# Tiles 4 and 5 load their first operands into the MLP's row rooms, and tiles 6 and 7 multiply in three passes

## The chip, the cores and the metric

The kernel runs on one core of one Trainium2 chip. The metric is the device time of one execution in microseconds (us). An execution taken by the profiler also has a span, from its first to its last instruction. TensorE (PE) multiplies, with a left operand loaded as weights (PEld); VectorE (DVE), ScalarE (ACT) and GpSimd (POOL) do the elementwise work; SyncE's queue (SP) issues nearly all loads and stores.

## The reference

One transformer block on a sequence of 1024 rows of width 1024, fp32 in and out. The hybrid mixer in the middle is left out here, since the change doesn't touch it.

```python
o   = hybrid_mixer(rms_norm(x, norm1_g), ...)        # two kinds of attention, [1024, 1024]
x   = x + o @ w_out                                  # w_out [1024, 1024]
h   = rms_norm(x, norm2_g)
q   = rms_norm((h @ w_xq).reshape(1024, 4, 128), xq_norm_g)      # 4 heads of 128
p   = softmax(q @ k.T * 128 ** -0.5)                 # k, v: 256 rows of a memory
x   = x + (p @ v).reshape(1024, 512) @ w_xo
h   = rms_norm(x, norm3_g)
out = x + square(relu(h @ w_ff_in)) @ w_ff_out       # inner width 4096
```

## The kernel before

The rows are eight tiles of 128. A first part projects them; then the attention of the tiles runs one after the other, and a second stream of work (`fill`) is laid between its instructions: the memory's keys and values, `between` for tiles 0 and 1 and for 2 and 3, the MLP of tiles 0 to 3 (`mlp`), and `between` for tiles 4 and 5. `between` is all that stands from the attention's rows to the MLP: it loads attention's rows o from DRAM (L948), multiplies them with w_out in four column chunks of 256, adds x (L938), norms (L311, L315), transposes the normed rows (L292), multiplies with w_xq in two chunks, each followed by the memory attention of its two heads (L984 to L1034), and multiplies with w_xo (L1044).

When attention is through, what is left of `between` for tiles 4 and 5 is merged with `between` for tiles 6 and 7; the latter uses a pool of its own, `d2`, opened in the room that attention leaves. After both comes `mlp_tail`, the MLP of tiles 4 to 7. Within each engine a scheduler of the framework then sets the order of the instructions, by its own model of times and by data dependences; an engine works through its list strictly in that order, SyncE's queue too.

There are two ways to multiply fp32. *Whole*: one matmul of fp32 operands, which the trace shows as two records. *Three passes*: both operands are split into a high part hi and a rest lo of a faster type, and hi·hi, hi·lo and lo·hi are added up, three matmuls of one record each. A weight piece is split by `split_w`: ScalarE copies hi (L251), GpSimd or VectorE subtracts to get lo (L256); at the tail these two take turns. Rows are split on the way out of PSUM by `split_ps` (L242 on ScalarE, L243 on VectorE). `between` multiplies whole for tiles 4 to 7; the MLP goes in three passes.

Tiles in SBUF come from rings: a tag with a number of buffers. In the pool of tiles 0 to 5 (`dn`) the tags `b4`, `whi` and `wlo` have four buffers each, and the MLP of tiles 0 to 3 uses the same ones as `between`: `b4` holds its residual rows until they are stored to the output (L1135), `whi` and `wlo` its split weights, `wraw` the raw ones. The MLP's transposed input rows lie in two rooms of their own, `xh` and `xl`, of 16 KB per partition each; after the last feature matmul nothing reads them.

Of the kernel before, what the change touches and what calls it, by code (L numbers as in the profile page):

```python
# [33 lines left out]
KG = 2  # L34
# [4 lines left out]
    "p2": {"x4": 5, "st": 2, "relu": 2, "whi": 4, "wlo": 4, "c8": 3, "c4": 1, "kraw": 4, "pc": 2},  # L39
    "dn": {"b4": 4, "h": 8, "relu": 2, "wraw": 2, "whi": 4, "wlo": 4},  # L40
    "res": {"b4": 4, "g": 2},
    "d2": {"b4": 2, "h": 8, "relu": 2, "whi": 4, "wlo": 4},
    "d3": {"h": 16, "relu": 2, "wraw": 4, "whi": 10, "wlo": 10},
}
PSUMS = {"p1": {"D": 4, "M": 3, "C": 1}, "main": {"S": 2, "PT": 2, "PV": 1, "D": 2, "M": 1}}
# [124 lines left out]
def build(nc, tc, I, C, out):  # L170
# [19 lines left out]
    def ring(pool, tag, shape, dt=F32):  # L190
        n = RINGS[pool.name if isinstance(pool.name, str) else "dn"][tag]
        return pool.tile(shape, dt, tag=tag, name=tag, bufs=n)
# [48 lines left out]
    def split_ps(src, hi, lo):  # L241
        s.activation(hi, src, AF.Copy)  # L242
        v.tensor_tensor(lo, src, hi, op=ALU.subtract)  # L243
# [74 lines left out]
    def weights(pool, xs, nk, wsrc, parts):  # L318

        w = sum(n for _, n in parts)  # L320
        for k0 in range(0, nk, KG):
            kn = min(KG, nk - k0)
            srcs, o = [], 0
            for c0, n in parts:
                srcs.append((lambda r, o=o, n=n: r[:, :, o:o + n],
                             wsrc[k0 * P:(k0 + kn) * P, c0:c0 + n].rearrange("(k p) n -> p k n", p=P)))
                o += n
            ws = load_w(pool, [P, kn, w], *srcs) if len(xs) == 2 else load_whole(pool, [P, kn, w], *srcs)
            for k in range(kn):
                yield [x[:, k, :] for x in ws]  # L330

    def gemm(pool, xs, nk, nt, wsrc, chunks, consume, begun=None):

        for ci, parts in enumerate(chunks):
            w = sum(n for _, n in parts)
            gr = begun if ci == 0 and begun else list(weights(pool, xs, nk, wsrc, parts))
            for t in range(nt):
                pt = pst(TAGS[pool.name][0], [P, w])
                for k in range(nk):
                    if len(xs) == 1:  # L340
                        mm(pt, xs[0](t, k), gr[k][0], k == 0, k == nk - 1)
                        continue
                    wh, wl = gr[k]
                    xh, xl = xs[0](t, k), xs[1](t, k)
                    mm(pt, xh, wh, k == 0, False)
                    mm(pt, xh, wl, False, False)
                    mm(pt, xl, wh, False, k == nk - 1)
                consume(ci, t, pt)
                yield nk * (5 - len(xs)) * w / 2400.0

    def row_by_row(pool, xs, nk, nt, wsrc, chunks, consume):

        gs = [list(weights(pool, xs, nk, wsrc, parts)) for parts in chunks]
        for t in range(nt):
            for ci, (parts, gr) in enumerate(zip(chunks, gs)):
                yield from gemm(pool, [lambda _, k, x=x, t=t: x(t, k) for x in xs], nk, 1, wsrc, [parts],
                                lambda c, u, pt, ci=ci, t=t: consume(ci, t, pt), gr)

    def xT(pool, nt, whole=False):

        parts = [pool.tile([P, DM // P, nt * P], F32 if whole else F32R, tag="x" + n, name="x" + n)
                 for n in ("h" if whole else "hl")]
        return (parts, [lambda t, k, x=x: x[:, k, t * P:(t + 1) * P] for x in parts],
                lambda t: [x[:, :, t * P:(t + 1) * P] for x in parts])
# [35 lines left out]
    def project(pool, part, late, st):  # L400
# [89 lines left out]

        def w_in(chunks, first, begun=None):
            return gemm(pool, xf, DM // P, nt, W["w_in"], chunks,
                        lambda ci, t, pt: consume(ci + first, t, pt), begun)

        def consume_kv(ci, t, pt):
            s.activation(kraw[t][:, DSA, :], pt[:, :64], AF.Copy)
# [441 lines left out]
            v.tensor_tensor(dst, pt, dst, op=ALU.add)  # L938
        return add_to

    def between(pool, t0, nt, x2s, keep, res=None, then=None):

        o_of = [ring(pool, "b4", [P, 8, P]) for t in range(nt)]
        rows, four = [lambda t, k: o_of[t][:, k, :]], [[(c * 256, 256)] for c in range(4)]
        first = list(weights(pool, rows, 8, W["w_out"], four[0]))
        for t in range(nt):
            for c in (1, 0):
                nc.sync.dma_start(o_of[t][:, c * 4:c * 4 + 4, :], oT_dr[t0 + t][c])  # L948
        x2 = [ring(res or pool, "b4", [P, DM]) for t in range(nt)]
        for t in range(nt):  # L950
            nc.sync.dma_start(x2[t], I["x"][0, (t0 + t) * P:(t0 + t + 1) * P, :])
        add_to = residual_add(x2)
        yield from gemm(pool, rows, 8, nt, W["w_out"], four, add_to, first)
        _, xf, xt_of = xT(pool, nt, True)

        gb2 = gain2(pool, W["norm2_g"])
        for t in range(nt):
# [1 line left out]
            yield 1.0  # L959

        kx, pts = [], {}
        xo = ring(pool, "b4", [P, 4, nt * P])

        def consume_q(ci, t, pt):
            if t == 0:
# [48 lines left out]
        def memory_values(ci, us, prs):  # L1014

            vh, vl = kx[1]
            n = len(us) * P
            split = []
            for h in range(2):
                p2 = pst(TAGS[pool.name][1], [P, 2, n])  # L1020
                for k in range(2):
                    for i, t in enumerate(us):
                        te.transpose(p2[:, k, i * P:(i + 1) * P], prs[t][:, h, k * P:(k + 1) * P], ident)
                ph, pl = ring(pool, "h", [P, 2, n], F32R), ring(pool, "h", [P, 2, n], F32R)
                split_ps(p2, ph, pl)
                split.append((ph, pl))
            pv = pst(TAGS[pool.name][0], [P, 2, n])
            for h, (ph, pl) in enumerate(split):
                hs = slice(h * P, (h + 1) * P)
                for k in range(2):  # L1030
                    mm(pv[:, h, :], vh[:, k, hs], ph[:, k, :], k == 0, False)
                    mm(pv[:, h, :], vl[:, k, hs], ph[:, k, :], False, False)
                    mm(pv[:, h, :], vh[:, k, hs], pl[:, k, :], False, k == 1)
            s.activation(xo[:, ci * 2:ci * 2 + 2, us[0] * P:us[0] * P + n], pv, AF.Copy)  # L1034

        yield from gemm(pool, xf, 8, nt, W["w_xq"], [[(0, 256)], [(256, 256)]], consume_q)

        if not keep and "res" in late:
# [3 lines left out]
            def add_to(ci, t, pt):  # L1042
                cs = slice(ci * 256, (ci + 1) * 256)
                v.tensor_tensor(kept[t][:, cs], pt, x2[t][:, cs], op=ALU.add)  # L1044
        by_tile = [lambda t, k: xo[:, k, t * P:(t + 1) * P]]
        last = (row_by_row if "res" in late else gemm)(pool, by_tile, 4, nt, W["w_xo"], four, add_to)
        yield from alternate(last, then()) if then else last
        for t in range(nt):
# [230 lines left out]
    def fill():  # L1279
        for part in range(1, len(PARTS)):  # L1280
            with tc.tile_pool(name="p2", bufs=1, reuse_waits="tile") as p2:
                yield from project(p2, part, late, st)
            projected.append(part)
        dn = dn_pool.__enter__()
        yield from memory(dn)
        yield 1, PACES[1]
        yield from between(dn, 0, 2, {}, False)
        yield 3, PACES[2]
        x2s, made = {}, {}
        yield from between(dn, 2, 2, x2s, True, None, lambda: pre_norms(dn, made, x2s))  # L1290
        yield 3, PACES[3]
        yield from mlp(dn, 0, 4, x2s, made)
        yield 5, PACES[4]
        yield from between(dn, 4, 2, late["x2s"], False)

    rest = fill()
    together(attend(aw, st), rest, projected)
# [41 lines left out]
```

## Time and profile before

| | us |
|---|---|
| median of 3 runs | 1752.03 (1748.72 to 1753.07) |
| profiled execution | 1755.7 |
| its span | 1753.9 |
| PE busy | 1671.0, 95% of the span |
| ACT busy | 1078.4, 61% |
| DVE busy | 967.4, 55% |
| POOL busy | 923.6, 53% |
| mean granted clock of PE | 0.98 of full |

The times in the rows are us from the start of the span, busy times are us and means of one instruction are ns. An instruction that had to wait shows in brackets how long its engine stood idle before it, and which instruction or DMA ended that. MLP of tiles 0 to 3 ends near 1216, attention near 1272, and the last stage, `mlp_tail`, takes over PE from about 1374 to the end.

### The profile page before, as it was taken

The page shows a single profiled execution, that of the slowest core. Times are in us where ns is not written, and L with a number is a line of the kernel's source. Part 1 is how long each engine was busy: PE and PEld are TensorE (multiplying, and loading weights), DVE is VectorE, ACT ScalarE, POOL GpSimd, SP SyncE. Part 2 cuts the span into 40 slices and gives each one's busy share as a digit, 9 for nine tenths or more (in the row PEclk, how much of TensorE's full clock was granted, in tenths as well). Part 3 has the DMA queues.
Part 4 walks back from the last instruction along what each step waited for, and adds up shares of the span by engine and source line. Part 5 has one row for each costly group of instructions (what it writes and reads, how often), then busy time and mean ns, then how long its engine had stood idle before and what let it go on. Part 6 is the DMA issues. An engine that isn't in the chain of part 4 may idle for free.

```text
span 1753.9 us, 27941 instructions
## 1 busy us (share of the span) xinstructions
PE 1671.0 (95%) x9294; PEld 1447.2 (83%) x9294; DVE 967.4 (55%) x2378; ACT 1078.4 (61%) x2713; POOL 923.6 (53%) x1073
## 2 busy tenths in 40 slices
PE   6998999899999999999999999998989899999999
PEld 6997987788788787888888888887978787888888
DVE  4565668766785886665657555554424544222243
ACT  5444796894698689857995589853313554333344
POOL 2354456554562445686667676673122565444456
PEclk9998999999999999999999999999999999999999
DMA  7434221545145221222122222125474454333353
GB/s 205 122 127 119 70 60 69 189 115 170 52 137 175 73 87 59 65 70 77 61 77 66 65 79 74 56 69 167 146 253 129 148 158 124 96 96 97 97 163 121
DMA packets 169520, 192.21 MB, mean 110 GB/s; under 512 B 24608, under 2 KB 134944, under 8 KB 169376
## 3 DMA queue, kind: packets, MB, share of 16 engines
q1 hardware_dynamic: 161296, 179.42, 33.1%
q0 software_dynamic: 7936, 10.49, 2.2%
q8 instruction: 74, 1.21, 0.3%
q14 instruction: 70, 0.57, 0.1%
q10 hardware_dynamic: 144, 0.52, 0.1%
HBM read 172.56 MB, written 17.83 MB: 109 GB/s over the span
## 4 chain that ended last, share of the span: by engine, by line
PE 62%; ACT 7%; DVE 5%; POOL 3%; issue 3%; DMA 2%; SPq 0%; POOLq 0%; ACTq 0%; DVEq 0%
PE psD L223 30%; PE psS L223 16%; PE psM L223 6%; PE psPV L223 4%; PE psPT L741 4%; ACT dmask L685 2%; POOL wlo L256 1%; ACT S L726 1%; POOL S L731 1%; DVE S L724 1%; ACT ph L242 1%; PE psM L292 1%; PE psPT L631 1%; ACT whi L251 1%; DMA whi<-in_w_out_dram 1%
## 5 line engine op out<-in xcount | busy, mean ns | idle before, releaser
L256 POOL TENSOR_TENSOR wlo<-wraw,whi 128x512 fp32r<-128x512 f32 (+1 forms) x233 | 321.0, 1384 | 268.6 <-ACT whi L251 261.2
L251 ACT ACTIVATE whi<-wraw 128x512 fp32r<-128x512 f32 x337 | 209.9, 627 | 191.2 <-PE psD L223 135.6
L223 PE MATMUL psD<-whi,h 128*128 128x512 f32 x688 | 237.1, 396 | 4.3 <-DVE b L1206 3.7
L256 DVE TENSOR_TENSOR wlo<-wraw,whi 128x512 fp32r<-128x512 f32 (+1 forms) x104 | 96.2, 925 | 186.9 <-ACT whi L251 186.8
L243 DVE TENSOR_TENSOR pl<-psPT,ph 128x512 fp32r<-128x512 f32 (+1 forms) x232 | 141.9, 620 | 72.4 <-ACT ph L242 70.9
L726 ACT ACTIVATE S<-S,mn 128x128 f32<-128x128 f32 (+7 forms) x192 | 142.7, 744 | 45.8 <-DVE mn L724 44.0
L242 ACT ACTIVATE ph<-psPT 128x512 fp32r<-128x512 f32 (+1 forms) x232 | 122.7, 539 | 75.9 <-PE psPT L741 72.1
L223 PE MATMUL psD<-wlo,xh 128*128 128x256 f32 (+1 forms) x608 | 164.7, 348 | 1.4 <-DMA wlo<-in_w_in_dram 1.4
L223 PE MATMUL psD<-whi,xh 128*128 128x256 f32 (+1 forms) x608 | 163.8, 346 | 2.0 <-DVE h L243 1.0
L731 POOL TENSOR_SCALAR S<-S,sums,gi 128x640 f32<-128x640 f32 (+7 forms) x128 | 113.9, 899 | 79.4 <-DVE sums L729 60.6
L223 PEld LDWEIGHTS psD<-whi,h 128*128 128x128 f32 x688 | 128.4, 188 | 30.3 <-DVE b L1206 4.4
L741 PE MATMUL psPT<-c_ident,S 128*128 128x128 f32 x816 | 134.4, 278 | 7.9 <-DVE cpl L243 3.3
L223 PE MATMUL psD<-wlo,h 128*128 128x512 f32 x344 | 136.1, 397 | 0.4 <-POOL wlo L256 0.4
L223 PE MATMUL psD<-xh,whi 128*128 128x512 f32 (+1 forms) x352 | 123.3, 350 | 0.0
L223 PEld LDWEIGHTS psD<-wlo,xh 128*128 128x128 f32 x608 | 114.6, 193 | 9.9 <-issue 1.5
L223 PE MATMUL psD<-xh,wlo 128*128 128x512 f32 (+1 forms) x352 | 122.3, 348 | 0.0
L223 PE MATMUL psD<-xl,whi 128*128 128x512 f32 (+1 forms) x352 | 122.1, 348 | 0.0
L223 PEld LDWEIGHTS psD<-whi,xh 128*128 128x128 f32 x608 | 113.0, 193 | 10.4 <-DVE Vd L243 1.4
L223 PE MATMUL psS<-K,qh 128*128 128x384 f32 (+3 forms) x288 | 112.3, 393 | 7.9 <-DVE mn L724 3.3
L741 PEld LDWEIGHTS psPT<-c_ident,S 128*128 128x128 f32 x816 | 98.3, 143 | 20.1 <-POOL S L731 5.5
L223 PE MATMUL psS<-K,ql 128*128 128x384 f32 (+3 forms) x288 | 98.1, 345 | 0.0
L685 ACT ACTIVATE dmask<-tkl,tkt 128x384 bf16<-128x384 uint16 (+5 forms) x96 | 84.3, 878 | 8.3 <-DVE tkl L683 6.7
(325 smaller groups left out, 4542.9 us busy)
## 6 DMA issues: line engine op xcount, KB each, us to landing
wraw<-in_w_ff_in_dram SPq DMA_DIRECT2D x44, 512.0 KB, 4.0
wraw<-in_w_ff_out_dram SPq DMA_DIRECT2D x44, 512.0 KB, 4.0
wraw<-in_w_ff_in_dram SPq DMA_DIRECT2D x64, 256.0 KB, 2.8
wraw<-in_w_ff_out_dram SPq DMA_DIRECT2D x64, 256.0 KB, 2.6
whi<-in_w_out_dram SPq DMA_DIRECT2D x32, 256.0 KB, 3.5
wlo<-in_w_out_dram SPq DMA_DIRECT2D x32, 256.0 KB, 4.3
wraw<-in_w_in_dram SPq DMA_DIRECT2D x24, 256.0 KB, 3.6
q<-st SPq DMA_DIRECT2D x12, 512.0 KB, 3.0
```

The source lines that it names most:

```text
L223: te.matmul(o, a, b, start=start, stop=stop)
L242: s.activation(hi, src, AF.Copy)
L243: v.tensor_tensor(lo, src, hi, op=ALU.subtract)
L251: s.activation(hi, raw, AF.Copy)
L256: (v if l == "v" else g).tensor_tensor(lo, raw, hi, op=ALU.subtract)
L292: te.transpose(pt[:, j, :], x_t[:, (c + j) * P:(c + j + 1) * P], ident)
L631: te.transpose(p2[:, h, :], qd[:, h, :, :].rearrange("p b d -> p (b d)"), ident)
L685: s.activation(mask, src, AF.Sign, bias=c, accum_out=over)
L724: v.tensor_tensor_reduce(out=dst, in0=sp, in1=m, scale=1.0, scalar=mn[:, 0:1] if i else 3e38, op0=ALU.add, op1=ALU.min, accum_out=low)
L726: s.activation(S, S, AF.Exp, bias=low, scale=-1.0, accum_out=sums[:, hh:hh + 1])
L731: g.tensor_scalar(Ss[hh], Ss[hh], sums[:, hh:hh + 1], 1.0 if gate is None else gate[:, hh:hh + 1], op0=ALU.mult, op1=ALU.mult)
L741: te.transpose(p2[:, j, hh, :], S[:, (c + j) * P:(c + j + 1) * P], ident)
```

## The change

Two edits. For tiles 4 and 5, `between` gets a `room`: attention's rows go into one half of the MLP's `xh`, the normed and transposed rows later into its other half, and the first two chunks of w_out into `xl`; all of it stays whole fp32, and the ring buffers are not asked for. For tiles 6 and 7, where `res` is given, `between` is `parted`: the rows o, the normed rows and the memory attention's output are split, w_out, w_xq and w_xo too, and all products go in three passes. The rings of `d2` get deeper for it. `gemm` takes its ready weights as a list of chunks. Lines from 336 on shift by up to 36; L984, L1010, L1023 and L1044 of before are L1013, L1039, L1052 and L1077 after.

```diff
-    "d2": {"b4": 2, "h": 8, "relu": 2, "whi": 4, "wlo": 4},
+    "d2": {"b4": 4, "xo": 2, "h": 8, "relu": 4, "wraw": 6, "whi": 8, "wlo": 8},
...
-            gr = begun if ci == 0 and begun else list(weights(pool, xs, nk, wsrc, parts))
+            gr = begun[ci] if begun and ci < len(begun) else list(weights(pool, xs, nk, wsrc, parts))
...
-    def between(pool, t0, nt, x2s, keep, res=None, then=None):
-
-        o_of = [ring(pool, "b4", [P, 8, P]) for t in range(nt)]
-        rows, four = [lambda t, k: o_of[t][:, k, :]], [[(c * 256, 256)] for c in range(4)]
-        first = list(weights(pool, rows, 8, W["w_out"], four[0]))
-        for t in range(nt):
-            for c in (1, 0):
-                nc.sync.dma_start(o_of[t][:, c * 4:c * 4 + 4, :], oT_dr[t0 + t][c])
+    def between(pool, t0, nt, x2s, keep, res=None, then=None, room=None):
+
+        parted, four = res is not None, [[(c * 256, 256)] for c in range(4)]
+        if parted:
+            o_of = [[ring(pool, "b4", [P, 8, P], F32R) for a in range(2)] for t in range(nt)]
+            rows = [lambda t, k, a=a: o_of[t][a][:, k, :] for a in range(2)]
+            first = [list(weights(pool, rows, 8, W["w_out"], four[0]))]
+            for t in range(nt):
+                for c in (1, 0):
+                    raw = ring(pool, "wraw", [P, 4, P])
+                    nc.sync.dma_start(raw, oT_dr[t0 + t][c])
+                    split_w(raw, *[o[:, c * 4:c * 4 + 4, :] for o in o_of[t]])
+        else:
+            if room:
+                o_of = [room[0][:, t] for t in range(nt)]
+                first = [[[room[1][:, c, k, :]] for k in range(8)] for c in range(2)]
+                for c in range(2):
+                    for k in range(0, 8, KG):
+                        nc.sync.dma_start(room[1][:, c, k:k + KG, :], W["w_out"][k * P:(k + KG) * P, c * 256:(c + 1) * 256]
+                                          .rearrange("(k p) n -> p k n", p=P))
+            else:
+                o_of = [ring(pool, "b4", [P, 8, P]) for t in range(nt)]
+            rows = [lambda t, k: o_of[t][:, k, :]]
+            if not room:
+                first = [list(weights(pool, rows, 8, W["w_out"], four[0]))]
+            for t in range(nt):
+                for c in (1, 0):
+                    nc.sync.dma_start(o_of[t][:, c * 4:c * 4 + 4, :], oT_dr[t0 + t][c])
...
-        _, xf, xt_of = xT(pool, nt, True)
+        if room:
+            xf, xt_of = [lambda t, k: room[2][:, k, t * P:(t + 1) * P]], lambda t: [room[2][:, :, t * P:(t + 1) * P]]
+        elif parted:
+            xs = [[ring(pool, "b4", [P, 8, P], F32R) for a in range(2)] for t in range(nt)]
+            xf, xt_of = [lambda t, k, a=a: xs[t][a][:, k, :] for a in range(2)], lambda t: xs[t]
+        else:
+            _, xf, xt_of = xT(pool, nt, True)
...
+            if parted:
+                split_ps(pv, *dst)
+            else:
+                s.activation(dst[0], pv, AF.Copy)
...
-        by_tile = [lambda t, k: xo[:, k, t * P:(t + 1) * P]]
+        by_tile = [lambda t, k, x=x: x[:, k, t * P:(t + 1) * P] for x in xo]
...
-        yield from between(dn, 4, 2, late["x2s"], False)
+        rows = dn.tile([P, 2, 8 * 256], F32, tag="xh", name="xh")
+        room = [rows[:, 0, :].rearrange("p (t k n) -> p t k n", t=2, k=8),
+                dn.tile([P, 2, 8, 256], F32, tag="xl", name="xl"), rows[:, 1, :].rearrange("p (k n) -> p k n", k=8)]
+        yield from between(dn, 4, 2, late["x2s"], False, None, None, room)
```

The lists of the engines are the same before and after up to the MLP's last group. SyncE's queue there, before: the last weight pieces of the MLP (w_ff_out into `wraw`), the stores of its output, and only then the rows o and w_out of tiles 4 and 5 (o_105 is attention's own output on its way to DRAM).

```order
L261 DMA wraw<-in_w_ff_out_dram 128x512 x3
L1135 DMA out_dram<-b_8330 128x512
...
L261 DMA wraw<-in_w_ff_out_dram 128x512 x2
...
L1135 DMA out_dram<-b_7200 128x512
L948 DMA b_14924<-o_99 128x512
L948 DMA b_14924<-o_98 128x512
L272 DMA wlo<-in_w_out_dram 128x2x256
L272 DMA whi<-in_w_out_dram 128x2x256 x2
```

And after, from the same place:

```order
L261 DMA wraw<-in_w_ff_out_dram 128x512 x3
L968 DMA xh<-o_99 128x512
L959 DMA xl<-in_w_out_dram 128x2x256 x3
L755 DMA o_105<-oc 64x2x128
L959 DMA xl<-in_w_out_dram 128x2x256
L261 DMA wraw<-in_w_ff_out_dram 128x512
L959 DMA xl<-in_w_out_dram 128x2x256
L261 DMA wraw<-in_w_ff_out_dram 128x512
L959 DMA xl<-in_w_out_dram 128x2x256 x3
L968 DMA xh<-o_98 128x512
...
L261 DMA wraw<-in_w_ff_out_dram 128x512
L1168 DMA out_dram<-b_8330 128x512
```

The loads of the rows and of w_out, now into `xh` and `xl` (L968, L959), have moved ahead of the last three of the six w_ff_out pieces and of the output's stores.

The second place is PE's list at the end of tiles 6 and 7. `psPT` and `psM` are PSUM banks of transposes, L292 transposes normed rows or q, `psS<-wlo,xh` is the end of w_xq's second chunk, `psS<-h` are scores and value products of the memory attention, and `psD` is the MLP tail. Before:

```order
L223 MATMUL psS<-wlo,xh 128x256 x2
L292 MATMUL psPT<-c_ident,relu 128x128 x2
L292 MATMUL psM<-c_ident,relu 128x128 x4
L223 MATMUL psS<-h 128x256 x2
L292 MATMUL psPT<-c_ident,relu 128x128 x2
L223 MATMUL psS<-h 128x256 x6
L292 MATMUL psM<-c_ident,relu 128x128 x4
L223 MATMUL psS<-h 128x256 x4
L223 MATMUL psD<-xh,whi 128x256
L223 MATMUL psD<-xh,wlo 128x256
L223 MATMUL psD<-xh,whi 128x256
L223 MATMUL psD<-xh,wlo 128x256
```

After, where `psS<-...xo` is w_xo:

```order
L223 MATMUL psS<-h 128x256 x10
L1052 MATMUL psPT<-c_ident,relu 128x128 x8
L223 MATMUL psS<-h 128x256 x2
L223 MATMUL psS<-whi,xo 128x256
L223 MATMUL psS<-wlo,xo 128x256
L223 MATMUL psS<-whi,xo 128x256 x2
...
L223 MATMUL psS<-h 128x256 x10
L223 MATMUL psS<-whi,xo 128x256
...
L223 MATMUL psS<-whi,xo 128x256
L292 MATMUL psM<-c_ident,relu 128x128 x12
L223 MATMUL psD<-xh,whi 128x256
```

The norm transposes of the MLP tail (`psM`) stood between the scores, and its features (`psD`) followed at once; now they stand behind the whole memory attention and behind w_xo's 96 matmuls.

ScalarE's list at that place, after (L242 evicts and L311 squares rows for the norm; 15847 and 15848 are the residual rows of tiles 4 and 5, 15308 and 15309 those of 6 and 7):

```order
L242 ACTIVATE xo<-psS 128x512
L311 ACTIVATE xh,nss<-b_15847 128x8x128
L311 ACTIVATE xh,nss<-b_15848 128x8x128
L311 ACTIVATE xh,nss<-b_15308 128x8x128
L251 ACTIVATE whi<-wraw 128x512 x2
L242 ACTIVATE xh<-psM 128x4x128
L311 ACTIVATE xh,nss<-b_15309 128x8x128
L251 ACTIVATE whi<-wraw 128x512 x5
L242 ACTIVATE xh<-psM 128x4x128
L251 ACTIVATE whi<-wraw 128x512 x3
L242 ACTIVATE xh<-psM 128x4x128 x2
```

Ten weight splits of the MLP tail and one square stand among the four evictions of `psM`; before, such splits stood there too, while PE had other matmuls.

## Rows read from the trace of the kernel before

**Rows 1.** The page: busy time, share of the span and instructions of each engine.

```profile
PE 1671.0 (95%) x9294; PEld 1447.2 (83%) x9294; DVE 967.4 (55%) x2378; ACT 1078.4 (61%) x2713; POOL 923.6 (53%) x1073
```

**Rows 2.** Windows: length, busy PE, PEld, DVE, ACT, POOL; PE clock, DMA share, GB/s.

```profile
1220.00:1230.00 10.00, 6.83 (x26) 5.80 (x27) 1.12 (x3) 0.78 (x2) 0.00 (x0) 0.66 1.08 380
...
1280.00:1290.00 10.00, 5.83 (x16) 4.64 (x17) 0.73 (x4) 1.92 (x8) 5.07 (x10) 0.66 1.11 371
...
1360.00:1370.00 10.00, 5.89 (x28) 4.32 (x27) 10.00 (x17) 6.37 (x14) 9.47 (x8) 0.87 0.87 288
```

**Rows 3.** Waits of PE, 1200 to 1310: us in all, times, longest.

```profile
PE psD L223 <- DMA whi<-in_w_out_dram: 6.5, 1, 6.5
```

**Rows 4.** Timeline of PE, 1177 to 1232: start, length, instruction, [idle before].

```profile
1177.41 0.39 PE L223 MATMUL psM<-xh,wlo 128*128 128x512 f32 x1
...
1185.56 0.40 PE L223 MATMUL psD<-wlo,h 128*128 128x512 f32 x1
...
1223.17 2.08 PE L223 MATMUL psD<-whi,b 128*128 128x256 f32 x4 [6.50 <-DMA whi<-in_w_out_dram]
1225.04 1.91 PE L223 MATMUL psD<-wlo,b 128*128 128x256 f32 x4
...
1231.00 1.03 PE L223 MATMUL psD<-whi,b 128*128 128x256 f32 x4
1231.87 1.03 PE L223 MATMUL psD<-wlo,b 128*128 128x256 f32 x4
```

**Rows 5.** Timeline of SyncE's queue, 1180 to 1212.

```profile
1180.32 5.45 SPq L261 DMA_DIRECT2D wraw<-in_w_ff_out_dram  x3
...
1211.66 2.09 SPq L948 DMA_DIRECT2D b<-o  x2
```

**Rows 6.** Timeline of ScalarE at 1183.

```profile
1183.40 0.63 ACT L251 ACTIVATE whi<-wraw 128x512 fp32r<-128x512 f32 x1 [0.54 <-DMA wraw<-in_w_ff_out_dram]
```

**Rows 7.** Timeline of PE in the MLP tail, 1389 to 1391.

```profile
1389.13 0.28 PE L223 MATMUL psD<-xh,whi 128*128 128x256 f32 x1
...
1390.54 0.28 PE L223 MATMUL psD<-xh,whi 128*128 128x256 f32 x1
```

**Rows 8.** Timeline of PE at attention's end, 1271 to 1285.

```profile
1271.56 0.28 PE L223 MATMUL psPV<-pl,Vd 128*128 128x256 f32 x1
...
1275.57 0.38 PE L292 MATMUL psM<-c_ident,relu 128*128 128x128 f32 x2
...
1284.50 2.08 PE L223 MATMUL psS<-whi,b 128*128 128x256 f32 x4 [2.52 <-DMA b<-o]
```

**Rows 9.** Timeline of VectorE at 1360.

```profile
1360.04 0.68 DVE L256 TENSOR_TENSOR wlo<-wraw,whi 128x512 fp32r<-128x512 f32 x1
```

**Rows 10.** Timeline of GpSimd at 1363.

```profile
1363.09 5.31 POOL L256 TENSOR_TENSOR wlo<-wraw,whi 128x512 fp32r<-128x512 f32 x3
```

**Rows 11.** Timeline of GpSimd at 1282.

```profile
1282.21 0.93 POOL L1010 TENSOR_SCALAR relu<-relu,xsum 128x256 f32<-128x256 f32 x2 [0.16 <-DVE xsum L1008]
```

**Rows 12.** Timeline of PE, 1347 to 1375.

```profile
1347.60 0.71 PE L1023 MATMUL psPT<-c_ident,relu 128*128 128x128 f32 x5
...
1362.74 0.38 PE L292 MATMUL psPT<-c_ident,relu 128*128 128x128 f32 x2
...
1374.42 0.36 PE L223 MATMUL psD<-xl,whi 128*128 128x256 f32 x1
```

**Rows 13.** Timeline of all engines, 1350 to 1359.

```profile
1350.46 0.60 ACT L242 ACTIVATE h<-psPT 128x512 fp32r<-128x512 f32 x1 [1.52 <-PE psPT L1023]
1351.09 0.69 DVE L243 TENSOR_TENSOR h<-psPT,h 128x512 fp32r<-128x512 f32 x1 [0.59 <-ACT h L242]
...
1355.91 1.06 ACT L311 ACTIVATE xh<-b 128x1024 fp32r<-128x1024 f32 x1 [4.85 <-PE psD L223]
1357.38 0.56 POOL L238 TENSOR_TENSOR nr<-nms,mhalf 128x1 f32<-128x1 f32 x1 [2.05 <-DVE nms L236]
1357.98 1.42 DVE L315 SCALAR_TENSOR_TENSOR relu<-b,nr,g 128x512 f32<-128x512 f32 x2 [0.74 <-POOL nr L238]
```

More of the change, by code (lines that the diff above doesn't have):

```diff
@@ L356, in row_by_row @@
                 yield from gemm(pool, [lambda _, k, x=x, t=t: x(t, k) for x in xs], nk, 1, wsrc, [parts],
-                                lambda c, u, pt, ci=ci, t=t: consume(ci, t, pt), gr)
+                                lambda c, u, pt, ci=ci, t=t: consume(ci, t, pt), [gr])
     def xT(pool, nt, whole=False):
@@ L492, in w_in @@
             return gemm(pool, xf, DM // P, nt, W["w_in"], chunks,
-                        lambda ci, t, pt: consume(ci + first, t, pt), begun)
+                        lambda ci, t, pt: consume(ci + first, t, pt), begun and [begun])
         def consume_kv(ci, t, pt):
@@ L961, in between @@
         kx, pts = [], {}
-        xo = ring(pool, "b4", [P, 4, nt * P])
+        if parted:
+            xo = [ring(pool, "xo", [P, 4, nt * P], F32R) for a in range(2)]
+        else:
+            xo = [ring(pool, "b4", [P, 4, nt * P])]
         def consume_q(ci, t, pt):
@@ L1033, in memory_values @@
                     mm(pv[:, h, :], vh[:, k, hs], pl[:, k, :], False, k == 1)
-            s.activation(xo[:, ci * 2:ci * 2 + 2, us[0] * P:us[0] * P + n], pv, AF.Copy)
+            dst = [x[:, ci * 2:ci * 2 + 2, us[0] * P:us[0] * P + n] for x in xo]
+            if parted:
+                split_ps(pv, *dst)
+            else:
+                s.activation(dst[0], pv, AF.Copy)
         yield from gemm(pool, xf, 8, nt, W["w_xq"], [[(0, 256)], [(256, 256)]], consume_q)
```

## The prediction, made before the changed kernel ran

> **What bounds the kernel now.** I read the page first: TensorE (PE) is busy for 95% of the span and no other engine for more than 61% [rows 1]. So an edit is worth what it takes from PE's list of work, or what it fills of the few places where PE stands still or works at the lower of its two clock levels (1.2 and 2.4 GHz). The windows of the last third show three such places [rows 2]: near 1220, near 1280, and from 1362 to 1374; between them PE is full. The list of PE's waits gives the first a name: 6.5 us for a chunk of w_out, ended by a DMA [rows 3].
>
> **Tiles 4 and 5.** In PE's rows the wait ends at 1223.17 [rows 4]. SyncE's queue says why the data is late: attention's rows are asked for at 1211.66 [rows 5], when the MLP's last down matmuls give back the ring tiles that the loads go into. The row rooms were last read at 1177.41, by the last feature matmul [rows 4]. With the change the loads go into them and can be issued from about 1178, over 30 us before anything else is missing, and w_out's matmuls lie among attention's. The wait goes: 6.5. After it PE works at the lower level: the first four records take 1.87 (1223.17 to 1225.04) where four such take 0.87 later (1231.00 to 1231.87) [rows 4]. That is 1.0, and I estimate as much again until the clock is back: 2.0. The amount of PE work is the same. What is late next: the order puts one row load and four w_out loads ahead of the last group's fourth w_ff_out piece, and more ahead of the later ones. These pieces are just in time today: issue from 1180.32 [rows 5], split at 1183.40 after 0.54 of waiting for the DMA [rows 6], multiplied at 1185.56 [rows 4]. The fourth piece stands behind five loads of 256 KB, 1.3 MB; the DMA moves 371 to 380 GB/s when it is asked for much [rows 2], so it is some 3.5 us later. Attention's matmuls, which stand between the MLP's in PE's list, cover most of that. I take 0.7; the bounds are 0 (all covered) and 4 (all later pieces late as well). Sum of this half: -6.5 - 2.0 + 0.7 = -7.8, bounds -8.5 and -4.5.
>
> **Tiles 6 and 7: the matmuls.** 128 products of 256 columns (64 of w_out, 32 of w_xq, 32 of w_xo) are multiplied as whole fp32 today, in two records each. Four records, two products, take 0.87 [rows 4], so 0.435 each and 55.7 in all. Three passes are 384 matmuls. The 12 steps between two rows of the MLP tail take 1.41 [rows 7], 0.1175 each: 45.1 in all. Saved: 10.6. This holds where PE is the bound.
>
> The Trainium skill (TensorE: Matmul & The Clock Gate, section Back-to-back issue gap) gives about N/2.4 + 2.5 ns for a single matmul at the upper level, 109 ns at 256 columns; the trace has 117.5 here, so the row decides. By the page the saving would be 13.8 and the sum 3.2 lower, still within what I call no change.
>
> **Splits and start.** The passes need 36 splits (32 weight pieces, 4 row halves), on ScalarE, then by turns on GpSimd and VectorE. The first product today starts at 1284.50, 12.9 after attention's last values at 1271.56 [rows 8]. In the new order w_xo's four loads stand ahead of w_out's in SyncE's queue, and the pieces are split before use: 0.63 on ScalarE [rows 6], 0.68 on VectorE when alone [rows 9]. Most of that lies beside loads still under way; I take +0.6 (0 to 3).
>
> Inside the stage the splits stand in order among the memory attention's norms, exponentials and evictions. One subtraction on GpSimd took 1.77 beside a full VectorE (5.31 for three [rows 10]); an eviction that stands behind two of these costs PE about 3. I take +3 (0 if the deeper rings let the splits run ahead, 10 if a third of the 18 subtractions on GpSimd, 6 x 1.77, falls on the path).
>
> **The loose ends.** The new order takes cover away at the end of this stage: the second column half of the memory attention, all of w_xo's 96 matmuls and then the MLP tail's first norms stand with no other work of PE beside them. Today features and norms of the MLP tail stand between them.
>
> First gap, from the end of w_xq's second product to w_xo's third row of weights. Pieces: from the transposes of q at 1275.57 to the last normalisation's end at 1282.21 + 0.93 = 1283.14 took 7.6 in the nearest uncovered case [rows 8, 11]; 8 transposes 1.1 (five take 0.71 [rows 12]); eviction 0.60 and subtraction 0.69 [rows 13]; 12 value matmuls 1.4; eviction 0.60. Sum 12.0. PE's own work in it is 4 transposes, 12 scores, 8 transposes and 12 value matmuls, 4.8. So 7.2 of standing still, and some 1.8 at the lower level behind it (as the 2.0 above): 9.0.
>
> Second gap, from w_xo's last matmul to the features. VectorE adds the last eighth (0.5), GpSimd's root 0.56, scaling of one half 0.71 (1.42 for two) and the hand-overs 0.4 [rows 13]; four transposes 0.5; eviction 0.6; then ScalarE has tile 7's square, 1.06 [rows 13], and five weight splits of 0.63 ahead of the next eviction, 4.2 together; eviction 0.6; three splits 1.9; two evictions and a subtraction 1.9; PE's transposes between, which have one bank, 1.0. Sum 12.9. PE's own 12 transposes are 2.2; 10.7 of standing still and 1.8 at the lower level: 12.5.
>
> Today's loose end goes with it: from 1362.74 to 1374.42 are 11.68 us [rows 12] with 32 records of about 0.1175, 3.8: a loss of 7.9.
>
> Sum of this half: -10.6 + 0.6 + 3 + 9.0 + 12.5 - 7.9 = +6.6. Bounds: -17.3 if the gaps cost no more than today's and starts and splits come nearly free, +16 if the splits take their upper value and the start its own.
>
> **Sum.** -7.8 + 6.6 = -1.2. The profiled execution took 1755.7 and its span 1753.9; it would be 1754.5. The median of the runs shown is 1752.03, 3.7 below it, so the forecast is 1750.8. A run of this kernel can tell about 0.3%, 5.3 us, from no change: the band is 1746.8 to 1757.3.
>
> **Rivals.** *Faster: the loose end stays as dear as today.* If the static order is worse than what happens (ScalarE's splits done early out of deep rings, the gaps closing to today's 7.9), 13.6 goes from the sum: -14.8, about 1737. Halfway it is 1744. For it: ScalarE is busy for 61% only [rows 1], and the window near 1360 today is full of splits [rows 2], which the deeper rings could spread. Against it: the rows behind the gaps depend on each other one by one, and no other PE work stands there. It decides when the gaps' surplus falls below about 9.
>
> *Slower: VectorE and GpSimd hold each other up at the splits.* One mechanism: both subtract weight pieces held in SBUF at the same time. From 1360 to 1370 today VectorE is busy for all of 10.00 and GpSimd for 9.47 [rows 2], GpSimd's three subtractions take 1.77 each [rows 10], and PE loses those 7.9. The change puts 18 subtractions more on each, which are 18 x 1.77 = 32 us on GpSimd. If a third of that delays PE (10.6, 7.6 above my 3) and the second gap is stretched by two subtractions (3), the sum is -1.2 + 10.6 = +9.4, about 1761. It decides once these two grow by 6.5 together. Against it: over a stage of some 90 us, 32 us is a load that fits.
> The Trainium skill (SBUF — State Buffer, section Who interferes with whom) says that a VectorE instruction with two SBUF inputs and a GpSimd one that reads SBUF take a shared port in turns, the second standing still for the whole of the first. GpSimd's 1.77 in the row agrees in sign.
>
> *The wait only moves.* If the room's loads hold back the last group's w_ff_out pieces at the upper bound, the first half gives -4.5 and the time is 1754: no change as well. For it: the pieces are just in time. Against it: the later ones wait for ring slots anyhow.
>
> **Chances.** The forecast with the moved wait in it, 0.45; the faster rival, whole or half, 0.33; the slower one 0.22. Half of the faster rival lies beyond 1746.8 by little, hence the low end at 1738; the high end takes the slower rival's price nearly whole, 1760. Faster by over 0.3%: 0.33; within: 0.45; slower: 0.22. The likeliest case alone spans 1746 to 1756.
>
> **What would show it.** Right in the first half: no wait of PE on w_out's DMA between 1200 and 1230, a window there granted 1.00, and w_out's loads issued before 1190. Wrong: new waits of PE on the w_ff_out pieces. Right in the second: w_out's, w_xq's and w_xo's records of tiles 6 and 7 step by 0.12 to 0.13; two stretches with a granted clock below 0.8 and PE under half busy, about 12 us each, the second on psM's transposes with ScalarE's splits before the releasing evictions. The forecast is wrong if PE is busy for over 80% across these stretches (faster), or if the splits' lo tiles release PE for more than 8 us in all (slower).

## The result and the profile after

The changed kernel takes 1765.17 us (median of 4 runs, 1764.32 to 1766.37) where before takes 1750.38 beside it (1747.28 to 1753.07): a ratio of 1.0086, 95% interval 1.0065 to 1.0106. It is slower by 14.8; the forecast was 1.2 faster, and 1765 lies beyond the range's upper end of 1760. Later runs of before, beside the experiments, have medians of 1752.4 to 1752.9, so some 12.5 is the better figure. Medians here and below are of the fast runs: two runs of before and one each of two experiments, which took from 1884 to 4196, are left out.

The profiled execution took 1764.47, its span 1762.3. The page's first line, beside [rows 1], says that busy shares have hardly moved.

```profile
PE 1672.1 (95%) x9422; PEld 1451.1 (82%) x9422; DVE 984.8 (56%) x2402; ACT 1100.0 (62%) x2749; POOL 951.3 (54%) x1091
```

PE's rows of the changed kernel, from the MLP's last feature matmul to the MLP tail, show where the halves part:

```profile
1173.97 0.39 PE L223 MATMUL psM<-xh,wlo 128*128 128x512 f32 x1
...
1259.10 0.28 PE L223 MATMUL psPV<-pl,Vd 128*128 128x256 f32 x1
...
1269.81 0.33 PE L1052 MATMUL psM<-c_ident,relu 128*128 128x128 f32 x1 [2.15 <-POOL relu L1039]
1275.01 0.58 PE L223 MATMUL psS<-whi,b 128*128 128x256 f32 x1 [4.87 <-ACT b L251]
1275.38 0.42 PE L223 MATMUL psS<-wlo,b 128*128 128x256 f32 x1
1275.60 0.84 PE L1052 MATMUL psM<-c_ident,relu 128*128 128x128 f32 x3
...
1361.41 0.93 PE L1052 MATMUL psPT<-c_ident,relu 128*128 128x128 f32 x2 [2.38 <-POOL relu L1039]
...
1381.99 0.66 PE L292 MATMUL psM<-c_ident,relu 128*128 128x128 f32 x4 [2.00 <-DVE relu L315]
1385.27 1.09 PE L292 MATMUL psM<-c_ident,relu 128*128 128x128 f32 x4 [2.62 <-DVE nms L236]
1389.84 1.08 PE L292 MATMUL psM<-c_ident,relu 128*128 128x128 f32 x4 [3.48 <-DVE xl L243]
1391.61 0.58 PE L223 MATMUL psD<-xh,whi 128*128 128x256 f32 x1 [0.69 <-ACT xh L242]
```

From the MLP's last feature matmul to attention's last value product were 94.15 (1177.41 to 1271.56, [rows 4, 8]); now they are 85.13 (1173.97 to 1259.10): 9.0 saved. From there to the end of the span were 482.3 (1753.9 - 1271.56) and are now 503.2 (1762.3 - 1259.10): 20.9 lost. Together +11.9 in the traces. That both are measured from a common instruction matters: what comes before it is the same code and starts 3.4 apart in these two executions.

The windows of the changed kernel (columns as in [rows 2]) show the first hole filled and four others:

```profile
1220.00:1230.00 10.00, 10.00 (x59) 8.96 (x59) 4.07 (x10) 3.30 (x6) 2.22 (x2) 1.00 0.43 148
...
1270.00:1280.00 10.00, 4.44 (x14) 3.46 (x14) 4.67 (x7) 6.13 (x12) 6.82 (x7) 0.59 1.10 372
...
1310.00:1320.00 10.00, 6.71 (x43) 5.95 (x43) 7.13 (x15) 7.63 (x18) 5.61 (x8) 0.81 0.47 145
...
1360.00:1370.00 10.00, 7.49 (x33) 6.11 (x34) 2.46 (x6) 4.87 (x13) 1.86 (x4) 0.66 0.00 1
...
1380.00:1390.00 10.00, 1.91 (x9) 1.33 (x10) 8.36 (x15) 7.77 (x15) 7.12 (x7) 0.72 0.20 67
```

Where 1220 to 1230 had 6.83 of busy time at a granted clock of 0.66, it is full. The first of the four, the start of tiles 6 and 7 (1270), stood before as well [rows 2, 1280]. Their norms (1310) are new. Their second memory attention (1360) and the passage to the MLP tail (1380) stand in place of the one loose end of before [rows 2, 1360].

To set prices I worked out PE's lost time: the length of a stretch less its matmuls at the steps that they have where PE is full and at the upper clock (0.216 for a record of a whole product, 0.118 for one of three passes at 256 columns, 0.232 at 512, 0.108 for a transpose). Idle time and the lower clock fall into it together. Time runs from attention's last value product.

```
us after attention's last product    before   after
 10 to  30  start of tiles 6, 7         4.4     9.9
 50 to  80  their norms                 0.0     7.6
 80 to 150  end of the stage            7.8    21.6
150 to 180  MLP tail, first groups      1.4     3.4
```

A trace lacks a few records; counted without them, single entries come out up to 0.7 higher.

### The profile page after: what moved, and what is told of

Read it like the earlier page. It is cut to its first block, busy times and chain, and to the rows that moved or that the text cites. A ratio compares the mean times of both kernels' runs of the same rounds, so it can differ in the third digit from the quotient of the medians.

```text
span 1762.3 us, 28307 instructions
## 1 busy us (share of the span) xinstructions
PE 1672.1 (95%) x9422; PEld 1451.1 (82%) x9422; DVE 984.8 (56%) x2402; ACT 1100.0 (62%) x2749; POOL 951.3 (54%) x1091
## 4 chain that ended last, share of the span: by engine, by line
PE 64%; DVE 5%; ACT 5%; POOL 4%; issue 3%; DMA 2%; SPq 0%; POOLq 0%; ACTq 0%; DVEq 0%
PE psD L223 31%; PE psS L223 16%; PE psM L223 7%; PE psPV L223 5%; PE psPT L741 4%; POOL wlo L256 1%; ACT dmask L685 1%; ACT S L726 1%; PE psM L292 1%; DVE S L724 1%; POOL S L731 1%; PE psPT L631 1%; DVE relu L315 1%; ACT ph L242 0%; DVE wlo L256 0%
## 5 line engine op out<-in xcount | busy, mean ns | idle before, releaser
L256 POOL TENSOR_TENSOR wlo<-wraw,whi 128x512 fp32r<-128x512 f32 (+1 forms) x249 | 343.6, 1387 | 270.3 <-ACT whi L251 262.0
L251 ACT ACTIVATE whi<-wraw 128x512 fp32r<-128x512 f32 x369 | 229.4, 627 | 199.5 <-PE psD L223 133.1
L256 DVE TENSOR_TENSOR wlo<-wraw,whi 128x512 fp32r<-128x512 f32 (+1 forms) x120 | 110.7, 923 | 193.7 <-ACT whi L251 193.6
L243 DVE TENSOR_TENSOR pl<-psPT,ph 128x512 fp32r<-128x512 f32 (+1 forms) x232 | 142.2, 620 | 69.4 <-ACT ph L242 67.5
L223 PE MATMUL psD<-whi,xh 128*128 128x256 f32 (+1 forms) x640 | 174.3, 352 | 1.8 <-DVE Vd L243 1.0
L223 PE MATMUL psD<-wlo,xh 128*128 128x256 f32 (+1 forms) x640 | 174.3, 351 | 0.8 <-DMA wlo<-in_w_in_dram 0.8
L242 ACT ACTIVATE ph<-psPT 128x512 fp32r<-128x512 f32 (+1 forms) x232 | 122.8, 539 | 73.1 <-PE psPT L741 68.5
L223 PEld LDWEIGHTS psD<-wlo,xh 128*128 128x128 f32 x640 | 121.4, 194 | 10.5 <-issue 0.9
L223 PEld LDWEIGHTS psD<-whi,xh 128*128 128x128 f32 x640 | 120.2, 195 | 11.3 <-DVE Vd L243 1.4
L223 PE MATMUL psD<-xh,whi 128*128 128x512 f32 (+1 forms) x352 | 123.4, 351 | 0.7 <-ACT xh L242 0.7
```

The source lines that it names most:

```text
L223: te.matmul(o, a, b, start=start, stop=stop)
L251: s.activation(hi, raw, AF.Copy)
L256: (v if l == "v" else g).tensor_tensor(lo, raw, hi, op=ALU.subtract)
```

## The experiments

Eleven kernels ran, one of them twice, each beside before on the same chip; ratios are against it, with 95% intervals.

**One half alone.** First tiles 4 and 5 with the room, and tiles 6 and 7 as before, run twice.

```diff
-        parted, four = res is not None, ...
+        parted, four = False, ...
```

> Only the first half of the change: tiles 4 and 5 get the room, tiles 6 and 7 multiply whole with the rings of before. Theory (the halves are independent, and the first is worth what the two traces show at attention's end, -9 to -12): 1738 to 1742 where before takes 1750. Rival (the freed time is only waited for later, at the start of tiles 6 and 7): 1746 or more.

> The first half alone once more, beside the run before on the same chip: 1744 to 1748 if its first result holds, and so the measure for whether three passes are worth anything.

Measured 1746.34, 0.9966 (0.9953 to 0.9979), and 1745.43, 0.9965 (0.9947 to 0.9982): 6.1 and 7.4 faster. The theory's 1738 to 1742 is missed; the first result lies at the edge of the rival's range. But the rival's place is not where the difference lies, since the loss at the start of tiles 6 and 7 is 4.6, nearly as before. In the traces the stretch up to attention's last product is 85.12 and 85.13, so it is 9.0 shorter than in the trace of before, but the rest is 485.9 and 485.8 long instead of 482.3. About 3.5 is given back later, some 2 of it in the old loose end (9.7 and 9.2 lost between 90 and 120, where before has 7.3). What makes that end dearer wasn't tried.

Then the second half alone, with tiles 4 and 5 as before.

```diff
-        yield from between(dn, 4, 2, late["x2s"], False, None, None, room)
+        yield from between(dn, 4, 2, late["x2s"], False)
```

> The second half alone: tiles 6 and 7 in three passes with the deep rings, tiles 4 and 5 without the room. Theory (the halves add up; the second costs 19 to 21 in the traces): 1770 to 1775. Rival (part of its cost is only there because the room starts tiles 6 and 7 earlier): 1758 to 1766.

Measured 1770.1, 1.0087 (1.0061 to 1.0114), 17.5 above the 1752.65 of before; its four runs go from 1761.5 to 1771.6. Within this spread the halves add up: +17.5 with -6.1 to -7.4 gives +10 to +11.4, where +12.5 was measured.

Its trace also shows how far one trace can be trusted for the price of a wait. Up to attention's last product PE's instructions and SyncE's loads are those of before, in the same order, yet PE waits 2.65 for the chunk of w_out and not 6.50 [rows 3, 4]:

```profile
1217.22 2.08 PE L223 MATMUL psD<-whi,b 128*128 128x256 f32 x4 [2.65 <-DMA whi<-in_w_out_dram]
```

The stretch is 89.84 here (1175.32 to 1265.16), where it is 94.15 in the trace of before. So the room's 9.0 holds against one execution, and against this one it is 4.7; the medians' 6.1 and 7.4 lie between.

**Where the loose ends come from.** The prediction took from the engines' lists that the second memory attention, w_xo and the tail's norms lose their cover, and did not ask why. The addresses in the built programs say it: the pool of tiles 6 and 7 lay from 151.4 KB per partition upwards, and with the deep rings it reaches down to 111.4. The MLP tail's pool ends at 141.3. So the two overlap now, and in the new lists everything of the tail stands behind everything of tiles 6 and 7 on PE, VectorE and ScalarE. Two tests. The deep rings without three passes, beside the room (the pool then starts at 123.4 KB, not at the 139 of the expectation):

```diff
     "d2": {"b4": 4, "xo": 2, "h": 8, "relu": 4, "wraw": 6, "whi": 8, "wlo": 8},
...
-        parted, four = res is not None, ...
+        parted, four = False, ...
```

> The room and the deeper rings of the pool of tiles 6 and 7, but these multiply whole, so there is no split and no third pass. Theory (the deeper rings make the pool reach from 139 KB down into the room of the MLP tail's pool, which ends at 141 KB, and the tail's norms and features then all come after the last product of tiles 6 and 7): 10 to 16 slower than the room alone, about 1753, with two stretches of PE half idle at the end of tiles 6 and 7. Rival (the cost lies in the splits, on VectorE and GpSimd): within 4 of the room alone, about 1741.

Measured 1760.45, 1.0046 (1.0032 to 1.0059): 14.1 above the room alone, with not one split more. Its windows have the same hole as the changed kernel's:

```profile
1380.00:1390.00 10.00, 2.27 (x11) 1.69 (x12) 9.55 (x14) 7.65 (x16) 7.99 (x7) 0.57 0.35 104
```

And a pair that differs in one buffer of the MLP tail. Both have shallow rings for tiles 6 and 7 and multiply with w_xo chunk by chunk; the first overlaps the tail's pool by 4 KB, the second not at all.

```diff
-    "d2": {"b4": 4, "xo": 2, "h": 8, "relu": 4, "wraw": 6, "whi": 8, "wlo": 8},
+    "d2": {"b4": 4, "xo": 2, "h": 8, "relu": 2, "wraw": 3, "whi": 4, "wlo": 4},
-        last = (row_by_row if "res" in late else gemm)(...)
+        last = (row_by_row if "res" in late and not parted else gemm)(...)
```

> The room and three passes for tiles 6 and 7, but with shallow rings (wraw 3, whi 4, wlo 4, relu 2) and w_xo chunk by chunk instead of all four loaded first; the pool then still reaches 4 KB into the MLP tail's room. Theory of the overlap: the loose ends stay, 1760 to 1768. Rival (the depth of the rings or the load order is what costs): clearly faster than the change, under 1757.

```diff
-    "d3": {"h": 16, "relu": 2, "wraw": 4, "whi": 10, "wlo": 10},
+    "d3": {"h": 16, "relu": 2, "wraw": 3, "whi": 10, "wlo": 10},
```

> As the run before, but the MLP tail has three raw weight buffers instead of four, so that its pool ends below that of tiles 6 and 7 (137.3 against 137.4 KB). Theory of the overlap: the tail's norms and features again lie among the memory attention of tiles 6 and 7, and it is 10 to 16 faster than its twin with four buffers, about 1750. Rival (splits on VectorE and GpSimd): within 3 of the twin, rather slower for the buffer that it lacks.

Measured 1766.59, 1.0078 (1.0063 to 1.0093), and 1750.74, 0.9987 (0.9976 to 0.9997): one buffer less makes it 15.9 faster, where the rival had 3 at most. PE's list at the end of the overlapping twin:

```
L223 MATMUL psS<-whi,xo 128x256
L292 MATMUL psM<-c_ident,relu 128x128 x12
L223 MATMUL psD<-xh,whi 128x256
```

and where the tail's norms stand in the clear one, between the transposes of the first memory attention:

```
L292 MATMUL psM<-c_ident,relu 128x128 x4
L1052 MATMUL psPT<-c_ident,relu 128x128 x2
L292 MATMUL psM<-c_ident,relu 128x128 x4
L1052 MATMUL psPT<-c_ident,relu 128x128 x6
```

PE in the windows from 1380 on, of the overlapping twin and then of the clear one, which keeps a loose end too, but a single one and earlier:

```profile
1380.00:1390.00 10.00, 5.38 (x44) 4.95 (x42) 6.07 (x14) 7.83 (x16) 5.09 (x6) 0.90 0.57 192
1390.00:1400.00 10.00, 5.83 (x26) 4.97 (x25) 6.45 (x8) 4.29 (x8) 6.46 (x5) 0.50 0.64 199
```

```profile
1340.00:1350.00 10.00, 4.03 (x18) 2.76 (x18) 8.79 (x14) 7.08 (x19) 7.81 (x9) 0.60 0.70 215
...
1380.00:1390.00 10.00, 9.84 (x55) 8.08 (x54) 5.87 (x9) 3.88 (x7) 4.14 (x4) 1.00 0.52 159
1390.00:1400.00 10.00, 10.00 (x88) 9.92 (x87) 4.68 (x10) 3.23 (x6) 4.29 (x4) 1.00 0.44 131
```

That the overlap is what puts the tail last is shown by the pair. The other built programs fit: where the pools overlap, no instruction of the tail stands ahead of the last one of tiles 6 and 7 on any engine; where they don't, 135 to 208 of PE's matmuls do. By which rule the scheduler does it was not seen.

**The norms of tiles 6 and 7.** All engines of the changed kernel at 1313:

```profile
1313.55 3.07 POOL L256 TENSOR_TENSOR wlo<-wraw,whi 128x512 fp32r<-128x512 f32 x2 [0.29 <-ACT whi L251]
1313.74 3.43 DVE L315 SCALAR_TENSOR_TENSOR relu<-b,nr,h 128x512 f32<-128x512 f32 x2
...
1315.55 0.66 PE L292 MATMUL psPT<-c_ident,relu 128*128 128x128 f32 x4 [2.21 <-DVE relu L315]
```

VectorE scales two halves in 3.43 while GpSimd subtracts two weight pieces; alone it took 1.42 [rows 13]. PE waits for it. All 36 lo parts of tiles 6 and 7 on VectorE take GpSimd out:

```diff
-    plan["w"] = PLAN_TAIL
+    plan["w"] = ("av",)
     d2 = d2_pool.__enter__()
...
     merge((rest, REST), (between(d2, 6, 2, x2s, True, res), 45.0))
+    plan["w"] = PLAN_TAIL
```

> The change, but the lo parts of all 36 splits of tiles 6 and 7 are subtracted on VectorE, none on GpSimd. Theory (VectorE's norm scaling took 3.4 for two beside GpSimd's subtractions instead of 1.4, and that held PE's transposes): the scaling goes back to 0.7 each, the loss at tiles 6 and 7's norms falls from 7 to 3 or 4, and the time by 2 to 4, to 1761 to 1763. Rival (VectorE has 18 subtractions more, 12 us, and they stand in its list ahead of the norms): no gain or slower, 1765 to 1772.

Measured 1758.35, 1.0036 (1.0024 to 1.0048): 6.8 below the change and more than the theory had, though VectorE has 18 subtractions more. VectorE's two pairs of halves in this kernel:

```profile
1308.10 1.41 DVE L315 SCALAR_TENSOR_TENSOR relu<-b,nr,h 128x512 f32<-128x512 f32 x2
...
1314.07 1.41 DVE L315 SCALAR_TENSOR_TENSOR relu<-b,nr,h 128x512 f32<-128x512 f32 x2 [1.02 <-POOL nr L238]
```

The loss between 50 and 80 falls from 7.6 to 2.9, and PE's waits for the scaled halves there from 3.2 to 0.4. But the loss at the start falls too, by some 2.5, and the lists move with the plan, so the 6.8 is not the hold-up's share alone; the 3.43 against 1.41 is. It is what the Trainium skill (SBUF — State Buffer, section Who interferes with whom) says of a VectorE instruction with two SBUF inputs beside a GpSimd one that reads SBUF: the later one stands still until the other is done. The trace agrees: 3.43 less 1.41 is 2.0, about one and a half subtractions. An instruction of VectorE on 128x2 elements shows a hold-up more plainly. It took 1.26 in the changed kernel, about as long as the subtraction of GpSimd beside it, and 0.16 with the lo parts on VectorE (at 1300.88):

```profile
1305.62 2.52 POOL L256 TENSOR_TENSOR wlo<-wraw,whi 128x512 fp32r<-128x512 f32 x2
1305.67 1.26 DVE L1019 TENSOR_SCALAR xsc<-xqr 128x2 f32<-128x2 f32 x1 [0.62 <-POOL xqr L238]
```

**The start of tiles 6 and 7.** ScalarE in the changed kernel, behind the exponentials of tiles 4 and 5:

```profile
1269.95 2.31 ACT L251 ACTIVATE whi<-wraw 128x512 fp32r<-128x512 f32 x4
1273.12 0.63 ACT L251 ACTIVATE b<-wraw 128x512 fp32r<-128x512 f32 x1 [0.86 <-DMA wraw<-o]
1274.32 0.63 ACT L251 ACTIVATE b<-wraw 128x512 fp32r<-128x512 f32 x1 [0.58 <-DMA wraw<-o]
```

and SyncE's queue, where four weight pieces and two row halves fill the six raw buffers, so that the next two rows wait until pieces are split:

```profile
1264.33 2.00 SPq L261 DMA_DIRECT2D wraw<-in_w_out_dram  x4
1266.43 0.90 SPq L951 DMA_DIRECT2D wraw<-o  x2
...
1271.40 1.30 SPq L951 DMA_DIRECT2D wraw<-o  x2
```

Two attempts, the rows first and then 1 MB less to load (this one leaves out the residual of tiles 6 and 7):

```diff
-            first = [list(weights(pool, rows, 8, W["w_out"], four[0]))]
             for t in range(nt):
                 for c in (1, 0):
                     raw = ring(pool, "wraw", [P, 4, P])
...
+            first = [list(weights(pool, rows, 8, W["w_out"], four[0]))]
```

> The change, but attention's rows of tiles 6 and 7 are loaded and split ahead of w_out's first chunk instead of behind it. Theory (at the start of tiles 6 and 7 PE stands still for the last split row, 4.9 in one wait with the memory attention of tiles 4 and 5 queued behind it): the wait shrinks to under 2 and the time falls by 2 to 5, to 1760 to 1763. Rival (the data of w_out is late by as much): within 1.5 of the change, 1764 to 1767.

```diff
+            if parted:
+                g.memset(x2[t], 0.0)
+            else:
+                nc.sync.dma_start(x2[t], I["x"][0, (t0 + t) * P:(t0 + t + 1) * P, :])
```

> The change, but the rows x of tiles 6 and 7 are set to zero by GpSimd instead of being loaded, so 1 MB less is asked for ahead of their weights and rows at attention's end; the residual of these tiles is left out. Theory (the start is late because the DMA moves some 370 GB/s for all of it): the first product starts 2.5 to 3 earlier after attention's last value product (13 instead of 15.9), the wait of 4.9 falls to about 2, and the time by 2 to 4, to 1761 to 1763. Rival (ScalarE's list of exponentials and splits sets the start): 15 to 16 as now, and 1764 to 1767.

Measured 1764.81, 1.0068 (1.0047 to 1.0089), and 1762.74, 1.0060 (1.0042 to 1.0078). The first theory falls: with the rows first, PE waits 6.1 for the other operand.

```profile
1275.80 0.80 PE L223 MATMUL psS<-whi,b 128*128 128x256 f32 x2 [6.12 <-ACT whi L251]
```

The second is unclear: the product starts 14.9 after attention's last one (1258.85 in that trace) instead of 15.9, between theory and rival, and the 2.4 of the medians are within what two sets of four runs may differ. It is no clean test either, because the lists moved: two of ScalarE's splits now stand ahead of an eviction of the memory attention, and PE waits 4.19 for that.

```profile
1270.32 1.68 PE L223 MATMUL psD<-h 128*128 128x256 f32 x6 [4.19 <-ACT h L242]
...
1273.78 0.58 PE L223 MATMUL psS<-whi,b 128*128 128x256 f32 x1 [1.77 <-ACT b L251]
```

The order of the loads alone is thus not what holds the start, and their amount isn't shown to be. One chain would fit the change and the rows-first kernel: ScalarE's first split begins behind the exponentials (1269.95 and 1271.97), a raw buffer comes free, the last loads are issued 1.45 later in both (1271.40 and 1273.42), and PE waits for their splits. More raw buffers than six would test it; no kernel had them, so the cause of the late start stays open.

**Versions put together.** The clear twin's rings with the rows first and the lo parts on VectorE; then, with the rows as in the change, six raw buffers (the tail's split rings at 8); and this with the rows first.

```diff
+    plan["w"] = ("av",)
-    "d3": {"h": 16, "relu": 2, "wraw": 4, "whi": 10, "wlo": 10},
+    "d3": {"h": 16, "relu": 2, "wraw": 3, "whi": 10, "wlo": 10},
```

> Clear of the tail's room (shallow rings, chunk by chunk, three raw buffers in the tail), with the rows loaded first and the lo parts on VectorE. Theory (overlap, late rows and the blocked scaling are what the three passes lost; they save about 9 of PE's work): 3 to 6 below the clear run's 1750.7 and level with or below the room alone, 1743 to 1747. Rival (the splits cost as much as the passes save, wherever they run): 1749 to 1753.

```diff
-    "d2": {..., "relu": 2, "wraw": 3, "whi": 4, "wlo": 4},
-    "d3": {..., "wraw": 3, "whi": 10, "wlo": 10},
+    "d2": {..., "relu": 2, "wraw": 6, "whi": 4, "wlo": 4},
+    "d3": {..., "wraw": 3, "whi": 8, "wlo": 8},
```

> Three passes for tiles 6 and 7, clear of the tail's room, lo parts on VectorE, six raw buffers for tiles 6 and 7 instead of three, paid for with the tail's split rings (8 instead of 10). Theory (ScalarE stood in line behind weight loads that had no raw buffer, and PE lost 4.7 some 50 us after attention's end): that loss goes to about 1, and it is 1740 to 1743, faster than the room alone. Rival (the splits themselves fill ScalarE and VectorE, or the tail misses its buffers): 1744 or more.

> The run before it with six raw buffers, and in addition the rows of tiles 6 and 7 loaded and split ahead of w_out. Theory (with the passes clear of the tail's room, what is left is the start, 6.9 lost between 10 and 20 us after attention's end against 4.6 where the rows came first): 2 below that run's 1744.9, so 1741 to 1744. Rival (whichever operand comes last, ScalarE's list behind the exponentials sets the start): 1744 to 1747.

Measured 1744.91, 0.9960 (0.9946 to 0.9975); 1744.87, 0.9955 (0.9939 to 0.9971); 1745.25, 0.9967 (0.9952 to 0.9981). The first came out as its theory had it. The other two missed theirs (1740 to 1743 and 1741 to 1744) and lie in their rivals' ranges: with six raw buffers the loss between 50 and 80 stays above 3, and the rows first don't make the start cheaper. All three beat before and the change, and none is told apart from the room alone: the medians are 0.2 to 1.5 below its two, and behind attention's last product the traces are 482.3 to 484.5 long, against 485.8 and 485.9. So three passes, freed of what they lost, are worth too little here for these runs to tell: some 9.8 less of PE's work against starts and norms that still cost more than with whole products (in the first of them 6.5 lost between 10 and 30 and 4.3 between 50 and 80, against 4.6 and 1.0 in the room alone).

## Why the prediction was wrong, step by step

- *Tiles 4 and 5, -7.8.* Right in kind: w_out's loads are issued from 1174.77 on, no wait on w_out's DMA is left between 1200 and 1230 and the clock there is 1.00. The list of PE's waits between 1170 and 1440 has no entry for a w_ff_out piece, so the 0.7 for late pieces was not needed. The size hangs on the one trace that it was read from: -9.0 against that execution, -4.7 against the one with a wait of 2.65, -6.1 and -7.4 in the runs of the room alone. That -7.8 comes close is in part luck.
- *The matmuls, -10.6.* Nearly right: w_xo's 12 steps take 1.415 (VectorE's adds follow each other by that), 0.118 each, and w_out's 0.12; 384 such are 45.9 instead of 45.1. Saved 9.8.
- *The loose ends, 9.0 + 12.5 - 7.9 = +13.6.* Right in place, in its waits and in the sum: lost time at the end of the stage grows from 7.8 to 21.6, which is 13.8. The waits are those foretold: the normalisation on GpSimd before the second values, then psM's three groups behind VectorE and ScalarE. The sum is in part luck: of the two gaps' price 17.9 was to be standing still and 3.6 the lower clock level, but PE stood still for some 14 (busy for 45.92 of the 60 from 1349.1 to 1409.1) and lost some 8 at the lower level. What the prediction missed is that this was no price of three passes: the rings' depth alone brings it, and one buffer takes it away.
- *First product, +0.6.* Too small: it starts 15.9 after attention's last product instead of 12.9 [rows 8], and PE's list has this product in front of three transposes of tiles 4 and 5, which wait the 4.87 with it. Lost time 9.9 instead of 4.4: +5.5, beyond my upper bound of 3. This is one of the two steps that failed. I had counted the loads as the cover of the splits, not that ScalarE comes to them only behind the exponentials; the rows show that order, but no run shows that it is the cause, which stays open.
- *Inside the stage, +3.* This is the other step that failed, by about as much: 7.6. I had looked for evictions and subtractions in the way of PE. What stood in the way most was VectorE's norm scaling, held by GpSimd's subtractions. The slower rival, with 1761 and a chance of 0.22, had the two engines hold each other up, but at their subtractions and not at the norms; it was to decide once this term and the second gap grew by 6.5 together. This term grew by 4.6 and the start by 4.9, while the second gap did not grow. Neither sign by which the forecast was to be wrong came: PE is not busy for over 80% across the gaps, and lo parts (L243, L256) release PE for under 5 in all, where 8 were named.
- *The tail.* +2.0 in its first groups, for which the sum had no term.
- *The lower bound of -17.3 for tiles 6 and 7* does not follow from its terms. With gaps as dear as before's and splits and start at nothing, -10.6 is left.

The list of PE's longest waits in the changed kernel carries these steps:

```profile
PE psS L223 <- ACT b L251: 4.9, 1, 4.9
PE psM L292 <- DVE xl L243: 3.5, 1, 3.5
PE psPT L292 <- DVE relu L315: 3.2, 2, 2.2
PE psD L223 <- DVE b L1239: 3.2, 2, 1.7
PE psM L292 <- DVE nms L236: 2.6, 1, 2.6
PE psPT L1052 <- POOL relu L1039: 2.5, 2, 2.4
```

In sum: -9.0, then -9.8 + 5.5 + 7.6 + 13.8 + 2.0 = +19.1 by lost time, where the trace has +20.9. Against the forecast of -1.2 the traces have +11.9, so 13.1 is missing. The start makes 4.9 of it and the inside of the stage 4.6, together 9.5; the tail makes 2.0, the matmuls' steps 0.8, the loose ends 0.2, and 1.8 the lost time doesn't explain, while the first half came out 1.2 cheaper.

## What to carry to other kernels

Before deepening a ring, look up where the pool then ends: a pool that reaches into the room of the stage behind it can push that whole stage back in every engine's list, and here a single buffer was worth 16 us. A faster way to multiply pays only where its operands are ready; count the splits on the engines that stand between the last stage and the first product, in the order in which these engines come to them. Put VectorE's elementwise work with two SBUF inputs and GpSimd's work that reads SBUF at different times, or on one of them. Price a wait for a DMA from more than one trace: here the same wait was 6.50 and 2.65.

## What the runs showed that was not expected

The stretch from the MLP's last feature matmul to attention's last value product is 85.12 or 85.13 in each of the traces with the room, while that first matmul stands between 1171.7 and 1177.5: executions differ by several us already in their first part. The clear twin with shallow rings ran from 1744.1 to 1754.3, and its profiled execution was the fastest; its trace would make it 2.5 faster after attention's end than the room alone, its median 4.4 slower. What differs between its runs was not found.
